# A decoder block on one core: when the first tile's expert rows are fetched

## The chip, the core and the metric

The kernel runs on one core of one Trainium2 chip. The metric is the device time of one execution in microseconds, median over runs. A core has a matrix engine (TensorE, PE in the profile; its weight loads are PEld), a vector engine (VectorE, DVE), an activation engine (ScalarE, ACT), a general engine (GpSimd, POOL) and a queue that only starts transfers (SyncE, SP). Each works through its own list of instructions in order. Where one instruction needs what another engine or a transfer makes, it waits, and all that stands behind it on its engine waits too.

## The reference, cut to what matters

One decoder layer on 512 tokens of width 1024, all in float32. The channel mixer at its end picks 128 experts for each token (8 heads with 16 each) out of 16384, and uses one row of u and one row of v for each:

```
h = rms_norm(x); proj = h @ w_in                # hgrn q,f,i,og | attn q,k,v | gate_a | gate_b
y_a = hgrn2_mixer(...);  y_b = dilated_attention_mixer(...)
merged = sigmoid(ga) * (y_a @ w_branch_a) + sigmoid(gb) * (y_b @ w_branch_b)
x = x + merged @ w_out
h2 = rms_norm(x)                                # peer_ffn(h2):
q = h2 @ w_q; scores against sub_keys; top 16 of 256 sums -> idx, gate = softmax(top scores)
hid = einsum('thkd,td->thk', u[idx], h2)        # 128 rows of u per token
a = gelu(hid) * gate
x = x + einsum('thk,thkd->td', a, v[idx])
```

## The kernel before

The 512 tokens are four tiles of 128. Tile 0 goes first and alone through the mixers, the output projection and the query projection; then tiles 1 to 3 go through the same steps together, as one `Front` with `split` set: each weight and each activation is cut into a high and a low half (line 98 on ACT makes the high half, line 99 the low one, on DVE or, one time in five among the w_in weights, on POOL), and each product is three matmuls (line 112).

The `Front` of tiles 1 to 3 runs these steps: the w_in products for HGRN2, attention and gates; `hgrn` and `attn` per tile; then `post`, which has four parts. W_AB multiplies the branch outputs by their weights, first all of branch a (line 479 into pairA), then all of branch b (line 479 into pairB, then line 481 and line 99 `xl<-pairA`). W_OUT is the output projection; line 494 adds its product to x, line 496 squares, line 500 sums, line 145 takes the reciprocal of the root. Line 512 then makes h2, three times: for tiles 1 and 2 in pairA, and for tile 3 in a buffer called h2g. Line 516 transposes h2 on PE, and W_Q is the query projection from it (line 112 again, `pp<-vs,wh`).

Weights stream through two buffers `w` of 512 KB (line 198, started by SP). After each such load the program calls `after_unit`, which for tiles 1 to 3 is `background`. This is where the work on tile 0's experts is put in.

For tiles 0 and 3 (`UG`), the rows of u are fetched one expert at a time: one indirect transfer started by POOL (line 648) brings 128 rows of 4 KB, one per token, into a buffer, and one DVE instruction (line 660) multiplies them by h2g and sums them into one column of `hid`. I call such a transfer of 512 KB with its product a row. A tile has 128 of them. There are four buffers, three named rq and one named row, used in turn. After the last row, line 664 (GELU, on ACT), line 665 and lines 553 to 557 (`thirds`) work the column sums up. `Pump` counts how many rows have been put in; `rows(n)` adds n to a credit and puts rows in until it is used up. The buffer h2g exists once: tile 3's h2 may be written into it when tile 0's last row has been multiplied.

A row of tile 0 has two conditions in the program of before: its buffer is free, and the load of weights with which it was put in has landed (`behind`, a dependence added by hand in `row`). Each load brings 1.8 rows; there are 50 loads of w_in and 16 in W_AB and W_OUT, and the rest of the 128 is put in by `before_h2`, ahead of line 512.

The order of instructions on each engine is set when the program is built, by a scheduler that takes the instructions whose inputs are ready by its own reckoning, in the order of the code where several are.

Of the kernel before, what the change touches and what calls it, by code (L numbers as in the profile page):

```python
# [18 lines left out]
P = 128  # L19
# [27 lines left out]

LPOOL = 5

ROWS_F = 1.8  # L50

NPRE, RING = 72, 56

# [20 lines left out]
def kernel(ctx: ExitStack, tc: tile.TileContext, x, wst, par, cst, cols, g2, keys, u, v, ut, vr, out):  # L74
# [22 lines left out]
    def halves(hi, lo, x, eng=None):  # L97
        nc.scalar.activation(hi, x, AF.Copy)  # L98
        (eng or nc.vector).tensor_tensor(out=lo, in0=x, in1=hi.bitcast(F32), op=ALU.subtract)  # L99
        return hi, lo  # L100
# [42 lines left out]
    def rstd_of(dst, ss, n):  # L143
        nc.scalar.activation(dst, ss, AF.Sqrt, bias=eps[:, 0:1], scale=1.0 / n)
        nc.vector.reciprocal(dst, dst)

    class Front:
# [318 lines left out]
                    for b in range(4):  # L466
                        nc.scalar.activation(dst[:, 2 * b:2 * b + 2], dst[:, 2 * b:2 * b + 2], AF.Sigmoid)

        def post(self, before_h2=lambda: None):

            ga, gb, N, n = self.ga, self.gb, self.N, self.n
            mT = ga
            if self.split:
                mT = [hp.tile([P, KC, NM], F32R, name=m)[:, :, :N] for m in ("hT", "xl")]
            for g, ks, y in ((ga, slice(0, 4), self.yaT), (gb, slice(4, 6), self.ybT)):
                for b in range(4):
                    c = slice(2 * b, 2 * b + 2)
                    for j, pt in self.proj_T(W_AB + b, y, ks):
                        nc.vector.tensor_mul(g[:, 2 * b + j], pt, g[:, 2 * b + j])
                    if g is gb:  # L480
                        (nc.vector if self.split else nc.gpsimd).tensor_tensor(out=ga[:, c], in0=ga[:, c], in1=gb[:, c], op=ALU.add)
                        if self.split:
                            halves(mT[0][:, c], mT[1][:, c], ga[:, c])
            g2b = fp.tile([P, 6 * S], F32, name="kT") if self.split else const.tile([P, KC * NU], F32, name="hL")
            g2b = g2b[:, :D]
            nc.sync.dma_start(out=g2b, in_=bass.AP(tensor=g2.tensor, offset=g2.offset, ap=[[0, P], [1, D]]))
            xt = hp.tile([P, NM // P, D], F32, name="pairB")[:, :n]
            ss = sp.tile([P, NM // P, 5], F32, name="ssx", bufs=1)[:, :n]
            scr = sp.tile([P, 256], BF16, name="scrx", bufs=1)
            nc.sync.dma_start(out=xt, in_=x[self.t0:self.t0 + N].rearrange("(t p) d -> p t d", p=P))  # L490
            for b in range(4):
                for ts, pt in self.proj_N(W_OUT + b, mT):
                    xs = xt[:, ts, b * 256:(b + 1) * 256]
                    nc.vector.tensor_add(xs, pt, xs)
                    for t in range(ts.start, ts.stop):
                        nc.scalar.activation(scr, xt[:, t, b * 256:(b + 1) * 256], AF.Square, accum_out=ss[:, t, b:b + 1])
                if b == 2:

                    nc.scalar.activation(root, ss[:, 0, b:b + 1], AF.Sqrt)
            nc.vector.tensor_reduce(out=ss[:, :, 4], in_=ss[:, :, :4], axis=AX.X, op=ALU.add)  # L500
            rstd_of(ss[:, :, 4], ss[:, :, 4], D)
            h2T = hp.tile([P, KC, NM], F32R if self.split else F32, name="vs")[:, :, :N]
            if self.split:
                h2T = h2T, hp.tile([P, KC, NM], F32R, name="xl")[:, :, :N]
                hu = self.hu = [const.tile([P, KC * NU], F32R, name=m).rearrange("p (k n) -> p k n", k=KC) for m in ("hH", "hL")]
            h2s = hp.tile([P, NM // P, D], F32, name="pairA")
            before_h2()
            for t, T in enumerate(self.tiles):
                h2 = h2s[:, t]
                if T in UG:  # L510
                    h2 = h2g[T] = const.tile([P, D], F32, name="h2g")
                self.last_h2 = nc.vector.scalar_tensor_tensor(h2, xt[:, t], ss[:, t, 4:5], g2b, op0=ALU.mult, op1=ALU.mult)
                for c in range(0, KC, 4):
                    pt = ps.tile([P, 4, P], F32, name="pt")
                    for k in range(4):
                        nc.tensor.transpose(pt[:, k], h2[:, (c + k) * P:(c + k + 1) * P], ident)
                    tk = slice(t * P, (t + 1) * P)
                    if self.split:
                        halves(*(h[:, c:c + 4, tk] for h in h2T), pt)
                    else:  # L520
                        nc.scalar.activation(h2T[:, c:c + 4, tk], pt, AF.Copy)
                    if T in UD:
                        d0 = UD.index(T) * P
                        halves(*(h[:, c:c + 4, d0:d0 + P] for h in hu), pt)

                nc.sync.dma_start(out=out[T * P:(T + 1) * P], in_=xt[:, t])
            rqs = [rq_pool.tile([P, PH, P], F32, name="rq") for _ in range(n)]
            for b in range(4):
                for j, pt in self.proj_T(W_Q + b, h2T):
                    for t in range(n):  # L530
                        nc.scalar.activation(rqs[t][:, 2 * b + j], pt[:, t * P:(t + 1) * P], AF.Copy)
            return rqs
# [109 lines left out]
    nrow, behind = [0], []  # L642
# [97 lines left out]
    rows, scat = Pump(), Pump()  # L740
# [4 lines left out]
    def mixers(f):  # L745
        f.proj_hgrn()
        for t in range(f.n):
            f.hgrn(t)
        f.proj_attn()
        for t in range(f.n):  # L750
            f.attn(t)
        f.proj_gates()

    f = Front(UG[:1], False, lambda load: None)
# [27 lines left out]
    row_places = [(rq_pool, "rq")] * 3 + [(gat, "row")]  # L782

    def background(load):
        behind[:] = [load]
        rows(min(ROWS_F, P - rows.done))

    f = Front(tuple(range(1, 4)), True, background)
    routing(0, rq0)
    rows.add(u_steps(UG[0]))  # L790
    mixers(f)
    rq1, rq2, rq3 = f.post(lambda: rows(2 * P))
    hH, hL = f.hu
    fctx.close()

# [129 lines left out]
def build(arrays):  # L925
    import concourse.bacc as bacc
    nc = bacc.Bacc("TRN2", target_bir_lowering=False, num_devices=1)
    args = {k: nc.dram_tensor(f"in_{k}_dram", a.shape, mybir.dt.from_np(a.dtype), kind="ExternalInput").ap()
            for k, a in arrays.items()}
    out = nc.dram_tensor("out_0_dram", (S, D), F32, kind="ExternalOutput").ap()  # L930
    with tile.TileContext(nc, schedule_with_timeline_sim=True) as tc:
        kernel(tc, **args, out=out)
    return nc
# [8 lines left out]
```

## Time and profile before

| | us |
|---|---|
| median of 3 runs | 1886.55 |
| lowest, highest | 1883.9, 1891.71 |
| the profiled execution | 1878.31 |
| its span | 1876.5 |
| PE busy in the span | 1684.9 (90%) |
| DVE busy | 1373.0 (73%) |
| ACT busy | 784.2 (42%) |
| POOL busy | 637.7 (34%) |

Between the profiled execution and its span lie 1.81 us. Times in the rows below count from the span's start. Tile 0's own front ends at about 200 us; the front of tiles 1 to 3, with tile 0's rows beside it, lasts from there to 664 us, and its query projection to 700 us. Then come the dense products with u (to about 1126 us) and those with v.

### The profile page before, as it was taken

The page shows a single profiled execution, that of the slowest core. Times are in us where ns is not written, and L with a number is a line of the kernel's source. Part 1 is how long each engine was busy: PE and PEld are TensorE (multiplying, and loading weights), DVE is VectorE, ACT ScalarE, POOL GpSimd, SP SyncE. Part 2 cuts the span into 40 slices and gives each one's busy share as a digit, 9 for nine tenths or more (in the row PEclk, how much of TensorE's full clock was granted, in tenths as well). Part 3 has the DMA queues.
Part 4 walks back from the last instruction along what each step waited for, and adds up shares of the span by engine and source line. Part 5 has one row for each costly group of instructions (what it writes and reads, how often), then busy time and mean ns, then how long its engine had stood idle before and what let it go on. Part 6 is the DMA issues. An engine that isn't in the chain of part 4 may idle for free.

```text
span 1876.5 us, 28078 instructions
## 1 busy us (share of the span) xinstructions
PE 1684.9 (90%) x10301; PEld 1496.5 (80%) x10301; DVE 1373.0 (73%) x2793; ACT 784.2 (42%) x1466; POOL 637.7 (34%) x502
## 2 busy tenths in 40 slices
PE   8998889788986599999999889999999999989995
PEld 7887888687775489988899778888888888877774
DVE  2114999956567748988899777787778877777874
ACT  3324443333342436662366793343334333323331
POOL 0000455732323301434444104433434334444431
PEclk9999989889997789999999869999999999999998
DMA  8776478766567724755666539999999988888885
GB/s 277 249 234 206 137 249 292 226 230 197 174 213 241 280 79 146 276 208 201 213 223 208 208 127 346 325 343 325 337 321 337 343 314 309 311 287 309 311 301 179
DMA packets 173386, 473.49 MB, mean 252 GB/s; under 512 B 14784, under 2 KB 62144, under 8 KB 173248
## 3 DMA queue, kind: packets, MB, share of 16 engines
q1 hardware_dynamic: 115840, 268.47, 41.9%
q0 software_dynamic: 55296, 201.35, 30.5%
q10 hardware_dynamic: 2112, 1.88, 0.3%
q8 instruction: 81, 1.33, 0.3%
q14 instruction: 57, 0.47, 0.1%
HBM read 442.80 MB, written 27.79 MB: 251 GB/s over the span
## 4 chain that ended last, share of the span: by engine, by line
PE 51%; DMA 24%; DVE 14%; issue 5%; ACT 3%; POOL 2%; DVEq 0%; ACTq 0%; POOLq 0%; SPq 0%
PE acc L873 19%; PE ph L112 15%; PE pp L112 10%; DMA Gc<-g_d 7%; DMA w<-in_wst_dram 6%; PE pg L711 5%; DMA rq<-in_u_dram,idx 4%; DMA row<-in_u_dram,idx 2%; DVE rq L660 2%; DVE wl L99 2%; DMA rowx<-in_u_dram,idx 2%; DMA rowx<-in_v_dram,idx 1%; DVE Gc L862 1%; ACT eg L705 1%; DVE row L660 1%
## 5 line engine op out<-in xcount | busy, mean ns | idle before, releaser
L873 PE MATMUL acc<-vl,ah 128*128 128x512 f32 x768 | 242.3, 395 | 8.2 <-DVE vl L869 8.1
L873 PE MATMUL acc<-vh,al 128*128 128x512 f32 x768 | 241.4, 392 | 0.0
L873 PE MATMUL acc<-vh,ah 128*128 128x512 f32 x768 | 224.7, 398 | 10.8 <-ACT vh L867 10.8
L648 POOL DMA_INDIRECT rowx<-in_u_dram,idx x96 | 125.0, 1302 | 221.0 <-ACT pre L822 61.6
L648 POOL DMA_INDIRECT rowx<-in_v_dram,idx x96 | 133.0, 1385 | 189.2 <-DVE h2g L679 90.8
L112 PE MATMUL ph<-hH,ul 128*128 128x256 f32 x640 | 183.5, 287 | 8.2 <-DVE ul L99 8.2
L112 PE MATMUL ph<-hH,uh 128*128 128x256 f32 x640 | 187.2, 293 | 3.6 <-ACT pre L822 3.6
L112 PE MATMUL ph<-hL,uh 128*128 128x256 f32 x640 | 183.1, 286 | 0.0
L112 PE MATMUL ph<-h,ub 128*128 128x256 f32 x768 | 178.3, 387 | 4.2 <-DMA ub<-in_ut_dram 4.1
L660 DVE SCALAR_TENSOR_TENSOR rq<-rq,h2g 128x1024 f32<-128x1024 f32 x96 | 128.1, 1338 | 66.6 <-DMA rq<-in_u_dram,idx 66.5
L873 PEld LDWEIGHTS acc<-vl,ah 128*128 128x128 f32 x768 | 144.3, 190 | 40.2 <-DVE vl L869 11.7
L98 ACT ACTIVATE ah<-Gc 128x384 fp32r<-128x384 f32 x128 | 67.0, 524 | 261.1 <-PE acc L873 255.9
L873 PEld LDWEIGHTS acc<-vh,ah 128*128 128x128 f32 x768 | 144.3, 191 | 39.6 <-ACT vh L867 12.2
L648 POOL DMA_INDIRECT rq<-in_u_dram,idx x96 | 108.6, 1132 | 196.9 <-DMA w<-in_wst_dram 71.0
L873 PEld LDWEIGHTS acc<-vh,al 128*128 128x128 f32 x768 | 145.0, 189 | 30.0
L98 ACT ACTIVATE uh<-ub 128x1024 fp32r<-128x1024 f32 x80 | 85.1, 1064 | 193.4 <-PE ph L112 154.8
L112 PEld LDWEIGHTS ph<-h,ub 128*128 128x128 f32 x768 | 146.1, 195 | 24.0 <-issue 4.7
L869 DVE TENSOR_TENSOR vl<-vb,vh 128x1024 fp32r<-128x1024 f32 x128 | 156.3, 1221 | 8.3 <-ACT vh L867 8.2
L711 PE MATMUL pg<-eg,e 128*128 128x128 bf16 x1152 | 147.1, 297 | 13.3 <-ACT eg L705 7.1
L867 ACT ACTIVATE vh<-vb 128x1024 fp32r<-128x1024 f32 x128 | 135.8, 1061 | 35.7 <-DMA vb<-in_vr_dram 34.7
L711 PEld LDWEIGHTS <-e 128*128 128x128 bf16 x1152 | 129.3, 119 | 25.4 <-DVE eg L701 9.8
L98 ACT ACTIVATE wh<-w 128x512 fp32r<-128x512 f32 x144 | 88.5, 628 | 141.8 <-PE pp L112 79.9
(292 smaller groups left out, 3949.5 us busy)
## 6 DMA issues: line engine op xcount, KB each, us to landing
ub<-in_ut_dram SPq DMA_DIRECT2D x128, 512.0 KB, 5.2
vb<-in_vr_dram SPq DMA_DIRECT2D x128, 512.0 KB, 7.0
w<-in_wst_dram SPq DMA_DIRECT2D x107, 512.0 KB, 4.9
g_d<-Gx SPq DMA_DIRECT2D x24, 960.0 KB, 4.3
Gc<-g_d SPq DMA_DIRECT2D x15, 1536.0 KB, 16.3
wh<-in_wst_dram SPq DMA_DIRECT2D x37, 256.0 KB, 5.2
wl<-in_wst_dram SPq DMA_DIRECT2D x33, 256.0 KB, 4.8
pairB<-in_x_dram SPq DMA_DIRECT2D x5, 512.0 KB, 5.3
```

The source lines that it names most:

```text
L98: nc.scalar.activation(hi, x, AF.Copy)
L99: (eng or nc.vector).tensor_tensor(out=lo, in0=x, in1=hi.bitcast(F32), op=ALU.subtract)
L112: nc.tensor.matmul(out, l, r, start=(k == 0 and i == 0), stop=(k == last and i == len(ops) - 1))
L648: d = nc.gpsimd.indirect_dma_start(out=r, out_offset=None, in_=src, in_offset=bass.IndirectOffsetOnAxis(ap=index, axis=0))
L660: nc.vector.scalar_tensor_tensor(r, r, 1.0, h2g[T], op0=ALU.mult, op1=ALU.mult, accum_out=hid[:, g, j:j + 1])
L705: nc.scalar.activation(eg[:, 2, :, q], e12[:, 1, :, q], AF.Copy, scale=pk3[:, VD.index(T), i + k + q:i + k + q + 1])
L711: nc.tensor.matmul(pt[:, q], e12[:, 0, :, q0 + q], eg[:, j, :, q0 + q], start=(j == 0), stop=(j == 2))
L862: nc.vector.tensor_mul(gsl[:, :ngu], a.rearrange("p (g t) -> p g t", t=GT), gsl[:, :ngu])
L867: behind[:] = [nc.scalar.activation(vH, vb, AF.Copy)]
L869: nc.vector.tensor_tensor(out=vL, in0=vb, in1=vH.bitcast(F32), op=ALU.subtract)
L873: nc.tensor.matmul(acc[t][c], l.rearrange("p g t -> p (g t)")[:, t * P:(t + 1) * P], r[:, c * 512:(c + 1) * 512], start=(b == 0 and i == 0 ...
```

## The change

Three edits. The dependence of a row on a load of weights is no longer set while tile 0's rows are put in. 2.8 rows go with each load instead of 1.8, so that the 128 rows are used up by the 46th of the 50 loads of w_in. And `rows(2 * P)`, which finishes the rows and adds the GELU and `thirds` of tile 0, stands between the mixers and `post`, instead of inside `post` ahead of h2. Line numbers of the changed program are lower by one from line 507 on, and by two after the edit at the end.

```diff
-ROWS_F = 1.8
+ROWS_F = 2.8
-        def post(self, before_h2=lambda: None):
+        def post(self):
             h2s = hp.tile([P, NM // P, D], F32, name="pairA")
-            before_h2()
             for t, T in enumerate(self.tiles):
     def background(load):
-        behind[:] = [load]
         rows(min(ROWS_F, P - rows.done))
     mixers(f)
-    rq1, rq2, rq3 = f.post(lambda: rows(2 * P))
+    rows(2 * P)
+    rq1, rq2, rq3 = f.post()
```

How the order of the instructions moves, at three places. First POOL, during attention: the starts of rows (L648 before, L647 after) and, between them, a low half that POOL makes (L99). In brackets stands what each waits for; DMAHW is a load by SP, DMASW an earlier row's landing, DVE the freeing of the buffer. Before:

```order
L99 TENSOR_TENSOR wl<-w,wh 128x512 [waits PE_49,Activation_49]
L648 DMA rq<-in_u_dram,idx 128x1024 [waits DMAHW6_49,DMASW2_49,DVE_49]
L648 DMA row<-in_u_dram,idx 128x1024 [waits DMASW3_49,DVE_49]
L648 DMA rq<-in_u_dram,idx 128x1024 [waits DMAHW7_49,DMASW4_49,DVE_49]
L648 DMA rq<-in_u_dram,idx 128x1024 [waits DMASW5_49,DVE_49]
L99 TENSOR_TENSOR wl<-w,wh 128x512 [waits PE_49,Activation_49]
```

The same place on POOL after:

```order
L99 TENSOR_TENSOR wl<-w,wh 128x512 [waits DMAHW4_49,PE_49,Activation_49]
L647 DMA row<-in_u_dram,idx 128x1024 [waits DMASW3_49,DVE_49]
L647 DMA rq<-in_u_dram,idx 128x1024 [waits DMASW4_49,DVE_49]
L647 DMA rq<-in_u_dram,idx 128x1024 [waits DMASW5_49,DVE_49]
L647 DMA rq<-in_u_dram,idx 128x1024 [waits DMASW6_49,DVE_49]
L647 DMA row<-in_u_dram,idx 128x1024 [waits DMASW7_49,DVE_49]
L99 TENSOR_TENSOR wl<-w,wh 128x512 [waits DMAHW6_49,PE_49,Activation_49]
```

No row waits for a load any more, and five rows stand between two low halves where four stood.

Second, DVE at the end of attention: L445 ends the last head of the last tile, L479 takes W_AB's products. Before:

```order
L445 TENSOR_SCALAR yb<-vg,m_4128 128x64
L479 TENSOR_TENSOR pairA<-pp,pairA 128x384
L99 TENSOR_TENSOR wl<-w,wh 128x512
L479 TENSOR_TENSOR pairA<-pp,pairA 128x384
L99 TENSOR_TENSOR wl<-w,wh 128x512
L660 SCALAR_TENSOR_TENSOR rq,hid<-rq,h2g 128x1024
L479 TENSOR_TENSOR pairA<-pp,pairA 128x384
```

The same place on DVE after:

```order
L659 SCALAR_TENSOR_TENSOR rq,hid<-rq,h2g 128x1024
L99 TENSOR_TENSOR wl<-w,wh 128x512
L479 TENSOR_TENSOR pairA<-pp,pairA 128x384
L445 TENSOR_SCALAR yb<-vg,m_4230 128x64
L659 SCALAR_TENSOR_TENSOR row,hid<-row,h2g 128x1024
L659 SCALAR_TENSOR_TENSOR rq,hid<-rq,h2g 128x1024
L99 TENSOR_TENSOR wl<-w,wh 128x512
L479 TENSOR_TENSOR pairA<-pp,pairA 128x384
```

Before the last L445, 94 rows stood on DVE; now 123 do. It comes after six of branch a's eight products instead of ahead of all of them, and 126 rows stand ahead of the last tile's `yb` halves.

Third, DVE between the end of W_OUT and W_Q: the sum of squares (L500), the reciprocal (L145), h2 (L512, after L511), its halves xl and hL (L99). Before:

```order
L500 TENSOR_REDUCE ssx<-ssx 128x3
L660 SCALAR_TENSOR_TENSOR rq,hid<-rq,h2g 128x1024
L145 RECIPROCAL ssx<-ssx 128x3
L512 SCALAR_TENSOR_TENSOR pairA<-pairB,ssx,kT 128x1024 x2
L660 SCALAR_TENSOR_TENSOR row,hid<-row,h2g 128x1024
L99 TENSOR_TENSOR xl<-pt,vs 128x4x128 x3
L99 TENSOR_TENSOR hL<-pt,hH 128x4x128
L660 SCALAR_TENSOR_TENSOR rq,hid<-rq,h2g 128x1024
L99 TENSOR_TENSOR hL<-pt,hH 128x4x128 x2
```

The same place on DVE after:

```order
L500 TENSOR_REDUCE ssx<-ssx 128x3
L145 RECIPROCAL ssx<-ssx 128x3
L511 SCALAR_TENSOR_TENSOR pairA<-pairB,ssx,kT 128x1024 x2
L511 SCALAR_TENSOR_TENSOR h2g<-pairB,ssx,kT 128x1024
L99 TENSOR_TENSOR xl<-pt,vs 128x4x128
L696 TENSOR_TENSOR e_6345<-iota,pk 128x1024
L696 TENSOR_TENSOR e_6367<-iota,pk 128x1024
L99 TENSOR_TENSOR xl<-pt,vs 128x4x128 x2
L700 TENSOR_TENSOR eg<-e_6345,pk 128x1024
L99 TENSOR_TENSOR hL<-pt,hH 128x4x128
L700 TENSOR_TENSOR eg<-e_6367,pk 128x1024
```

No row stands there any more, tile 3's h2 follows the other two at once, and four instructions of a later step (L696, L700) have moved in among the halves. In W_AB's branch b and in W_OUT no row is left either.

## Rows read from the trace of the kernel before

**Rows 1.** Busy us by stretch: PE, PEld, DVE, ACT, POOL; granted clock, DMA share, GB/s.

```profile
230.00:372.00 142.00, 116.55 (x826) 108.83 (x824) 135.76 (x280) 51.66 (x105) 89.00 (x66) 0.86 0.76 250
372.00:556.00 184.00, 163.11 (x1162) 143.22 (x1163) 111.31 (x225) 69.71 (x141) 56.18 (x55) 0.93 0.62 204
556.00:664.00 108.00, 63.52 (x380) 58.35 (x379) 82.05 (x135) 32.16 (x66) 32.88 (x29) 0.76 0.70 241
664.00:700.00 36.00, 36.00 (x197) 35.01 (x198) 10.65 (x19) 14.39 (x42) 0.00 (x0) 0.95 0.30 103
```

**Rows 2.** The chain of waits from 556 to 664 us, by line.

```profile
by line: DMA w<-in_wst_dram 24.9%; DMA rq<-in_u_dram,idx 24.8%; issue 12.4%; DVE rq L660 8.0%; DVE wl L99 5.6%; POOL rq L648 4.1%; DVE xl L99 3.7%; DVE row L660 2.3%; DVE pairA L512 2.3%; DVE h L830 2.0%; DVE hL L99 1.7%; DVE pairA L481 1.6
```

**Rows 3.** DVE's time in line 660 by stretch (two instructions each row), clock, DMA.

```profile
250.00:300.00 50.00, 23.85 (x40) 0.97 0.82 280
230.00:372.00 142.00, 67.78 (x100) 0.86 0.76 250
372.00:556.00 184.00, 57.59 (x91) 0.93 0.62 204
556.00:664.00 108.00, 38.83 (x64) 0.76 0.70 241
```

**Rows 4.** Waits from 372 to 556 us: total us, times, longest.

```profile
POOL rq L648 <- DMA w<-in_wst_dram: 50.7, 8, 8.4
POOL row L648 <- DMA w<-in_wst_dram: 14.7, 4, 6.6
...
DVE rq L660 <- DMA rq<-in_u_dram,idx: 47.4, 17, 5.1
DVE row L660 <- DMA row<-in_u_dram,idx: 10.9, 6, 3.7
```

**Rows 5.** Transfers from 300 to 372 us, then 372 to 430: size, median us to landing.

```profile
w<-in_wst_dram SPq DMA_DIRECT2D x8, 512.0 KB, 6.7
...
w<-in_wst_dram SPq DMA_DIRECT2D x10, 512.0 KB, 4.9
rq<-in_u_dram,idx POOLq DMA_INDIRECT x12, 5.8
```

**Rows 6.** POOL in order of time: start, us, what [idle before, releaser].

```profile
226.77 1.45 POOL L648 DMA_INDIRECT rq<-in_u_dram,idx  x1 [1.36 <-DVE rq L660]
```

**Rows 7.** PE in order of time, W_AB's branch b to W_Q.

```profile
558.46 0.51 PE L112 MATMUL pp<-yb,wh 128*128 128x384 f32 x2
...
578.67 0.47 PE L112 MATMUL pp<-wh,hT 128*128 128x256 f32 x1 [3.37 <-DVE pairB L479]
...
633.41 0.28 PE L112 MATMUL pp<-wh,xl 128*128 128x256 f32 x1
633.53 0.28 PE L112 MATMUL pp<-wl,hT 128*128 128x256 f32 x1
...
663.53 0.69 PE L112 MATMUL pp<-xl,wh 128*128 128x384 f32 x1 [1.32 <-DVE xl L99]
```

**Rows 8.** DVE in order of time, end of W_OUT to W_Q.

```profile
635.55 1.22 DVE L660 SCALAR_TENSOR_TENSOR rq<-rq,h2g 128x1024 f32<-128x1024 f32 x1
...
642.75 1.22 DVE L660 SCALAR_TENSOR_TENSOR rq<-rq,h2g 128x1024 f32<-128x1024 f32 x1 [2.94 <-DMA rq<-in_u_dram,idx]
...
644.11 2.48 DVE L512 SCALAR_TENSOR_TENSOR pairA<-pairB,ssx,kT 128x1024 f32<-128x1024 f32 x2
...
656.72 1.22 DVE L660 SCALAR_TENSOR_TENSOR row<-row,h2g 128x1024 f32<-128x1024 f32 x1
...
657.98 1.28 DVE L512 SCALAR_TENSOR_TENSOR h2g<-pairB,ssx,kT 128x1024 f32<-128x1024 f32 x1
...
659.38 2.29 DVE L830 TENSOR_TENSOR h<-hH,hL 128x2048 f32<-128x2048 f32 x1
661.59 1.29 DVE L697 TENSOR_TENSOR e<-iota,pk 128x1024 bf16<-128x1024 bf16 x2
```

**Rows 9.** ACT's wait for weights from 556 to 664 us.

```profile
ACT wh L98 <- DMA w<-in_wst_dram: 21.8, 7, 8.2
```

## The prediction

> **What bounds the kernel now.** I read the busy time by stretch first. The change touches only tile 0's rows, and they lie between 224 and 658 us, so I cut that time at the steps of the program. From 664 us on PE has no gap in the query projection [rows 1], so what the front gains or loses should reach the end. From 372 to 556 us (last w_in products, attention, gates, W_AB's branch a) PE is busy 163.1 of 184 us. From 556 to 664 us (branch b, W_OUT, h2) it is busy only 63.5 of 108 us [rows 1], at a granted clock of 0.76 in the mean, that is for about half of the time at the lower of its two levels, 1.2 GHz and not 2.4. These 44.5 idle us are the largest hole in the front.
>
> Then the chain of waits in this hole. A quarter of it is loads of weights, a quarter transfers of rq rows, a further tenth the product of rows on DVE; PE does not appear among its first eleven entries [rows 2]. So this stage is held up by things that DVE does in order between the operands that PE needs.
>
> Third, the waits of 372 to 556 us. POOL stood 50.7 + 14.7 = 65.4 us at the start of a row, until a load of weights had landed. DVE stood 47.4 + 10.9 = 58.3 us in front of a row's product, until the row had landed [rows 4]. DVE is busy 111.3 of 184 us there [rows 1], so 72.7 us are idle, and 58.3 of them are these waits: a row starts late, because it waits for a load, and is then waited for.
>
> **What the change moves.** Line 660 runs 91 times from 372 to 556 us and 64 times from 556 to 664 us; with two instructions a row that is 45.5 and 32 rows [rows 3]. In the order after, 29 more rows stand ahead of the last attention head, and no row is left behind the start of branch b but the last one or two. So the stretch from 372 us to branch b gets about 45.5 + 29 = 75 rows, and what follows up to W_Q none.
>
> **Part 1, the rows brought forward: +4 us.** One row costs DVE 57.6 / 45.5 = 1.27 us [rows 3], so 29 rows add 36.8 us to DVE's 111.3: 148 of 184 us. With the 14.4 us that DVE idles for other reasons (72.7 - 58.3) that is 162.5, and 21.5 us are left for waits on rows, 0.29 us each. Whether this holds depends on how fast four buffers can be turned over, now without the wait for a load. Floor: POOL starts a row 1.4 us after DVE has freed its buffer [rows 6], the row lands 5.8 us after its start [rows 5], DVE takes 1.27; that is 8.5 us for four buffers, 2.1 us a row, and 75 rows need 159 us. Slowest row of the trace: from 230 to 372 us, where most rows did not wait for a load, 50 rows went through in 142 us, 2.84 us each, but with DVE busy 135.8 of the 142 us [rows 1, 3]; 75 rows at that pace need 213 us. In between stands 250 to 300 us with 20 rows in 50 us, 2.5 us each [rows 3]. DVE has more room after 372 us than there, so I take 2.5: 75 x 2.5 = 187.5 us against 184, a cost of 4 us. The ends are kept: 159 us would leave PE as the bound, with its 163 us of work, so that at most some 10 us could be won; 213 us would cost 29. Transfers can carry it: 204 GB/s x 184 us is 37.5 MB, 29 rows of 0.524 MB add 15.2, and 52.7 MB in 188 us are 280 GB/s, as much as the transfers moved from 250 to 300 us, then at a share of 0.82 [rows 3].
>
> **Part 2, branch b: -3 us.** It lasts from 558.5 to 578.7 us [rows 7]. Eight products of 6 matmuls, at about the 0.17 us that one of 384 columns takes (half as much again as the 0.12 us of one of 256 [rows 7], an estimate), are 8 to 9 us of PE work. After the change the last rows and tile 0's GELU fall into its beginning, so I count 3 of the 20 us, with 0 and 8 as bounds.
>
> **Part 3, W_OUT: -14 us.** It lasts from 578.7 to 633.7, 55 us [rows 7]. Its 4 x 8 x 3 x 3 = 288 matmuls follow each other every 0.12 us at the full clock [rows 7], 34.6 us, which is the floor. The nearest stretch is the query projection behind it, the same eight loads of weights and no rows: 36 us with PE without a gap [rows 1]. I add 5 us, because unlike that one W_OUT begins with operands that DVE is still making (its first matmul had waited 3.4 us) [rows 7]: 41 us. Bounds are 36 and 55.
>
> **Part 4, from W_OUT to W_Q: -12 us.** From PE's last matmul at 633.7 to the query projection in earnest at 663.5 are 30 us [rows 7]. DVE has eight rows in there (the first at 635.55, the last at 656.72), 8 x 1.22 = 9.8 us, and one waits 2.9 us for its transfer while the reciprocal stands behind it [rows 8]. Line 512 for tile 3 comes 11.4 us after the other two began, because its buffer is tile 0's h2 and the last rows still read it. All that goes: 12.7 us. Line 830 (2.3 us) moves from ahead of the last xl to behind it, and four instructions of 0.65 us (half of the pair at 661.6) move ahead of it, two of which were ahead before [rows 8]: about -1. What is late next is the chain itself: sum, root, three h2, transposes, ten halves of 0.65 us. I take 12, with 8 and 15 as bounds.
>
> What I cost at nothing: the GELU's change of ACT table comes once more, but ACT is busy only 32 of 108 us there [rows 1], and PE has three buffers of products in front of it; uncovered I would not expect it to cost more than one row's product (1.2 us, an estimate). POOL starts the same 128 rows.
>
> **Sum.** 4 - 3 - 14 - 12 = -25 us. The profiled execution took 1878.31 (span 1876.5 and 1.8 around it); with 25 less it would take 1853. It lies 8.2 us below the median of the three runs, so against the median the forecast is 1886.55 - 25 = 1861.5 us.
>
> **Rivals.**
>
> First, the rows' pace becomes the bound. At 2.84 us a row part 1 costs 29 us, and 29 - 29 = 0: about 1886.5. For it: with 75 rows in order on DVE, attention's small steps and the low halves of weights stand behind each row that is not there yet, and eight products of branch a now stand among some thirteen rows. Against it: that pace was measured with DVE full of routing work [rows 1, 3].
>
> Second, slower. A row's wait on DVE stays what it was, 58.3 / 45.5 = 1.28 us, because the transfer itself is what takes long and not the wait ahead of it. Then 75 rows wait 96 us, and the stretch takes 162.5 + 96 = 258.5 us, 74.5 more; less 29 that is +45, about 1932. It decides from 0.67 us of wait a row on, where 162.5 + 75 x 0.67 = 213. For it: loads landed in 6.7 us instead of 4.9 when rows came densely [rows 5], so transfers do lengthen each other. Against it: from 230 to 372 us, where rows were hardly held back, DVE idled 6.2 us in all [rows 1], 0.12 us a row.
>
> The Trainium skill bears on this ("DMA: Bandwidth & Descriptors", section "Queues, rings and completion order"): each transfer engine goes round the queues that have work and changes between them only at whole packets, so a row and a load in flight together stretch each other. By that rule alone, with a row always beside a load, landing would go towards twice the undisturbed time, and this rival would be the forecast; the medians of 4.9 and 6.7 us agree in direction and are less than a doubling [rows 5].
>
> Third, only part 4 is won. ACT waited 21.8 us for weights between 556 and 664 us [rows 9]; if the loads, and not DVE, set the pace of branch b and W_OUT, parts 2 and 3 give nothing and -12 + 4 = -8 remains: about 1878.5. For it speaks the quarter of the chain that is loads [rows 2]; against it the same eight loads in the query projection, where PE had no gap [rows 1].
>
> **How the numbers follow.** The forecast gets 0.60, the first rival 0.17, the slower one 0.10, the third 0.13. What a measurement of this kernel can tell from no change is about 0.5%, 9.4 us. The forecast lies beyond it; a part of the third rival (0.06) does too, so faster gets 0.66, within 0.5% gets 0.23, slower 0.11 with a little from the first. The forecast's own range, with the bounds of its parts, goes from about 1845 (parts 2 to 4 at 6, 19, 14, part 1 at -3) to 1877. To leave out no more than two in ten the range must take in the third and most of the first: 1845 to 1888.
>
> **What the profile after would show.** Right: POOL's waits for loads of weights at row starts gone; the last row's product before about 562 us instead of 657; DVE's waits for rows between 372 and 560 us below some 30 us in sum; W_OUT in about 41 us with PE's clock near full; h2 of tile 3 directly behind the other two, and W_Q beginning near 638 us instead of 663. Wrong: attention and branch a ending 20 us or more later than at 558 us, with DVE waiting for rq and row transfers before every product; or W_OUT still lasting 50 us with ACT waiting for loads. The forecast would also fail if the dense stage behind 700 us gave the time back, which PE's full stretch at 664 us does not suggest.

## The result, and the profile after

| | before | after |
|---|---|---|
| median, us | 1886.47 (4 runs) | 1834.5 (4 runs) |
| lowest, highest | 1883.9, 1891.71 | 1826.47, 1845.72 |
| the profiled execution | 1878.31 | 1845.72 |
| its span | 1876.5 | 1843.9 |

The ratio is 0.9725, with a 95% interval from 0.967 to 0.9781: 52 us faster where 25 were forecast, and below the forecast's range (1845 to 1888). The two profiles differ by only 33 us, because that of before is of an execution quicker than any of the four timed ones, and that of after is the slowest of its four. A second profile of the changed kernel, taken with the experiments, is of an execution of 1830.23 us, 48 less than the profile of before. I use both.

The stages after, cut at the same steps of the program as in [rows 1] (w_in from 372 us on, branch a, branch b, W_OUT, from there to W_Q, W_Q; columns as there):

```profile
372.00:512.80 140.80, 135.43 (x1000) 121.23 (x998) 119.36 (x230) 54.82 (x119) 84.92 (x68) 0.97 0.88 302
512.80:553.40 40.60, 28.78 (x207) 24.62 (x205) 34.19 (x68) 16.68 (x29) 22.44 (x18) 0.83 0.88 297
553.40:567.40 14.00, 11.95 (x49) 10.86 (x49) 13.60 (x27) 6.87 (x10) 0.00 (x0) 0.76 0.48 157
567.40:608.80 41.40, 37.69 (x288) 36.42 (x288) 19.57 (x34) 17.17 (x38) 0.00 (x0) 0.96 0.44 141
608.80:623.50 14.70, 5.76 (x26) 4.75 (x25) 12.57 (x20) 9.44 (x25) 0.00 (x0) 0.63 0.42 143
623.50:659.60 36.10, 36.10 (x199) 34.88 (x198) 12.32 (x16) 12.43 (x35) 0.00 (x0) 0.96 0.30 103
```

And of before with the same cuts, w_in and W_OUT:

```profile
372.00:537.20 165.20, 145.90 (x1060) 126.93 (x1061) 99.03 (x202) 60.14 (x126) 49.64 (x49) 0.93 0.60 200
...
578.70:633.80 55.10, 42.78 (x288) 40.41 (x288) 38.32 (x62) 16.91 (x37) 16.91 (x15) 0.81 0.71 240
```

W_OUT takes 41.4 us instead of 55.1, and DVE has half as much to do in it. The w_in products end 24 us earlier on the clock of the trace, although DVE did more in them; PE stands still for 5 us there instead of 19, and its granted clock is 0.97 in the mean instead of 0.93. Branch a, though, takes 40.6 us instead of 21.3: the rows that were brought forward stand in it now.

The waits from 372 to 553 us after, against [rows 4] (total us, times, longest):

```profile
ACT wh L98 <- DMA w<-in_wst_dram: 44.3, 15, 7.7
POOL rq L647 <- DVE rq L659: 36.0, 28, 2.9
...
DVE rq L659 <- DMA rq<-in_u_dram,idx: 15.9, 15, 2.7
...
DVE row L659 <- DMA row<-in_u_dram,idx: 4.5, 5, 1.4
```

POOL waits for the freeing of buffers, and no longer for loads; DVE's waits for rows are 20.4 us, where they were 58.3. The largest entry is now ACT's wait for loads (20.1 us in the stretch of [rows 4]), whose transfers share the time with the rows'.

DVE's time in a row's product after, against [rows 3], and the transfers from 378 to 512 us, against [rows 5]:

```profile
378.00:512.00 134.00, 74.28 (x111) 0.97 0.89 305
372.00:550.00 178.00, 99.22 (x153) 0.94 0.87 300
```

```profile
w<-in_wst_dram SPq DMA_DIRECT2D x22, 512.0 KB, 7.2
rq<-in_u_dram,idx POOLq DMA_INDIRECT x42, 6.8
row<-in_u_dram,idx POOLq DMA_INDIRECT x14, 6.5
```

153 instructions in 178 us are 76.5 rows, one each 2.33 us. Loads and rows land later than before, at a DMA share of 0.89. In the second profile, from 378 to 510 us, the delay is smaller:

```profile
w<-in_wst_dram SPq DMA_DIRECT2D x22, 512.0 KB, 6.2
rq<-in_u_dram,idx POOLq DMA_INDIRECT x42, 6.4
row<-in_u_dram,idx POOLq DMA_INDIRECT x13, 6.1
```

The end of W_OUT on DVE after, against [rows 8] (start, us, what, idle before and its releaser), and the start of W_Q on PE, against [rows 7]:

```profile
611.71 0.17 DVE L500 TENSOR_REDUCE ssx<-ssx 128x3 f32<-128x12 f32 x1 [1.12 <-ACT scrx L496]
612.25 0.18 DVE L145 RECIPROCAL ssx<-ssx 128x3 f32<-128x3 f32 x1 [0.36 <-ACT ssx L144]
612.46 2.48 DVE L511 SCALAR_TENSOR_TENSOR pairA<-pairB,ssx,kT 128x1024 f32<-128x1024 f32 x2
614.86 1.28 DVE L511 SCALAR_TENSOR_TENSOR h2g<-pairB,ssx,kT 128x1024 f32<-128x1024 f32 x1
```

```profile
623.45 1.01 PE L112 MATMUL pp<-vs,wh 128*128 128x384 f32 x2
```

The third h2 stands directly behind the first two.

What scatters from run to run is mostly outside the stages of the change. From W_Q's end to the end of the span there are 1176.7 us in the profile of before, 1184.3 and 1173.8 in the two of the changed kernel, and 1169 to 1192 in those of the experiments. So I compare profiles by one length, the front: from the first product of a tile 0 row to the end of W_Q. Before it is 475.4 us (224.4 to 699.8), after 429.7, and in the second profile 429.1. The change gave 46 us in there. Most kernels below have one profile each, so how far the front of one program scatters is known only from these two. That the medians differ by 52 has nothing in these stages to show for the last 6 us; the profiled run of before lies 8 us under its median.

### The profile page after: what moved, and what is told of

It reads as the page before. It is cut to its first block, busy times and chain, and to the rows that moved or that the text cites. A ratio compares the mean times of both kernels' runs of the same rounds, so it can differ in the third digit from the quotient of the medians.

```text
span 1843.9 us, 28097 instructions
## 1 busy us (share of the span) xinstructions
PE 1672.6 (91%) x10301; PEld 1485.2 (81%) x10301; DVE 1374.9 (75%) x2793; ACT 783.4 (42%) x1467; POOL 653.9 (35%) x502
## 4 chain that ended last, share of the span: by engine, by line
PE 49%; DMA 23%; DVE 18%; issue 5%; ACT 3%; POOL 2%; DVEq 0%; SPq 0%; POOLq 0%; ACTq 0%
PE acc L872 16%; PE ph L112 13%; PE pp L112 12%; DMA Gc<-g_d 7%; PE pg L710 5%; DMA w<-in_wst_dram 3%; DMA row<-in_u_dram,idx 3%; DMA rq<-in_u_dram,idx 3%; DMA rowx<-in_u_dram,idx 2%; DVE rq L659 2%; DVE wl L99 1%; DVE row L659 1%; DVE Gc L861 1%; DMA rowx<-in_v_dram,idx 1%; DVE h2g L678 1%
## 5 line engine op out<-in xcount | busy, mean ns | idle before, releaser
L647 POOL DMA_INDIRECT rowx<-in_v_dram,idx x96 | 136.3, 1420 | 204.1 <-DVE h2g L678 93.4
L647 POOL DMA_INDIRECT rowx<-in_u_dram,idx x96 | 125.9, 1312 | 215.8 <-issue 57.0
L647 POOL DMA_INDIRECT rq<-in_u_dram,idx x96 | 118.6, 1236 | 99.3 <-DVE rq L659 62.4
```

Of the source, the lines that this page charges most:

```text
L647: d = nc.gpsimd.indirect_dma_start(out=r, out_offset=None, in_=src, in_offset=bass.IndirectOffsetOnAxis(ap=index, axis=0))
```

## The experiments

The change does three things at once: it takes away a wait, it puts more rows behind each load, and it moves `rows(2 * P)`. The order on the engines moves with them. Theory A: the gain comes from where the rows stand in the order (the prediction's parts 3 and 4). Theory B: it comes from the waits for loads themselves. The expectations name these, and C and D for the rows that are left.

| run | rows a load | waits for loads | rows on DVE at last head | front, us | ratio to before, 95% |
|---|---|---|---|---|---|
| before | 1.8 | yes | 94 | 475.4 | 1 |
| e3_rest_before_post | 1.8 | yes | 96 | 464.8 | 0.9942 (0.9914 to 0.9969) |
| w20_wait_2 | 2.0 | yes | 110 | 446.9 | 0.9851 (0.9807 to 0.9895) |
| e2_wait_28 | 2.8 | yes | 123 | 430.0 | 0.9700 (0.9666 to 0.9735) |
| n1_order_of_before | 1.8 | no | 96 | 441.7 | 0.9765 (0.9731 to 0.98) |
| v20_no_wait_2 | 2.0 | no | 108 | 423.7 | 0.9691 (0.9653 to 0.973) |
| e1_no_wait | 1.8 | no | 123 | 436.4 | 0.9725 (0.9687 to 0.9763) |
| a_again (the change) | 2.8 | no | 123 | 429.1 | 0.9704 (0.967 to 0.9738) |

The edit of n1 and v20 reaches further than the others. It stands in `row`, which tile 3 uses too, behind 700 us, with rows that wait for a result of ACT. POOL's largest waits of that kind before, from 700 to 1830 us:

```profile
POOL rowx L648 <- ACT pre L822: 68.8, 21, 10.5
POOL rowx L648 <- ACT ah L98: 40.0, 16, 11.8
```

In n1 and v20 no such wait is left. So their ratios hold more than tile 0's rows, and what the wait for loads cost is read from their fronts.

### Each edit alone

**e1_no_wait.** The dependence alone is removed:

```diff
     def background(load):
-        behind[:] = [load]
```

> Only the dependence on loads is removed; still 1.8 rows with each load, and the last rows put in ahead of line 512. Each engine's order comes out as in the changed kernel (123 rows ahead of the last attention head, none behind branch b). Theory A (the gain comes from where the rows stand in the order: none in branch b, W_OUT and ahead of h2): as fast as the changed kernel, 0.972 of before, -52 us; W_OUT in about 41 us. Theory B (it comes from the turnover of the four buffers, which the waits for loads slowed): the same, -52 us, since the waits are gone. Rival C (the larger credit, 2.8, is what brings the rows forward): 1.0 of before, W_OUT in about 55 us.

Measured 1838.23 us, 0.9725. This edit alone gives the change's order and, within the intervals, its gain (39 of the 46 us of the front). Theories A and B both expected that; rival C falls.

**e2_wait_28.** Only the number of rows:

```diff
-ROWS_F = 1.8
+ROWS_F = 2.8
```

> Only 2.8 rows with each load instead of 1.8; the rows still wait for their load, and rows(2 * P) stands where it stood before. DVE's order is that of the changed kernel. Theory A (order): W_OUT about 41 us, no row ahead of h2, most of the gain: -40 to -52 us. Theory B (turnover): a row's wait on DVE stays 1.28 us as before; by the prediction's second rival 75 rows then wait 96 us and the stretch from 372 us to branch b takes about 258 us instead of 184: slower than before by up to 45 us in sum, or at best 0 if half of the waits go.

Measured 1831.37 us, 0.9700: also the whole gain, with the dependence on loads still in the program. Theory B expected a loss or nothing. The waits of POOL from 372 to 556 us in this run:

```profile
POOL rq L648 <- DVE rq L660: 38.5, 27, 3.3
...
POOL row L648 <- DVE row L660: 9.7, 7, 2.0
```

No wait for a load is left among them, where before had 65.4 us [rows 4]. With 2.8 rows a load the four buffers cannot keep up, rows fall behind, and the load that a row names has landed before its buffer is free. So this run brings the rows forward and loses the waits at once, as the change does, and does not tell theory A from B.

**e3_rest_before_post.** Only the third edit:

```diff
-    rq1, rq2, rq3 = f.post(lambda: rows(2 * P))
+    rows(2 * P)
+    rq1, rq2, rq3 = f.post()
```

> Only rows(2 * P) is moved to between the mixers and post; 1.8 rows with each load, each behind its load, as before. DVE has 96 rows ahead of the last head (before 94), 119 by W_OUT's beginning and all 128 by its end; none stands ahead of h2. By the prediction's part 4: -12 us, W_OUT still near 55 us. If the waits for loads were what cost the stretch up to branch b 19 us (the run without waits in the order of before), POOL's waits stay near 65 us from 372 to 556 us and nothing is won there. If -30 us or more come, the waits were not it, but the order alone.

Measured 1875.62 us, 0.9942, 11 us less, as part 4 had it (12). W_OUT and the stretch behind it in its profile:

```profile
586.50:640.70 54.20, 43.38 (x289) 41.20 (x289) 41.52 (x74) 20.75 (x44) 19.85 (x15) 0.81 0.79 274
640.70:656.40 15.70, 5.71 (x25) 4.74 (x25) 12.83 (x22) 10.63 (x26) 0.00 (x0) 0.61 0.38 134
```

No row stands ahead of h2, and the 30 us to W_Q have become 16. W_OUT, with 17 rows in it, has hardly moved. Up to branch b it took 7 us longer than before (340.9 us from the first row's product, 334.0 before); the front is 11 us shorter in sum. POOL still waited for loads, 47 us:

```profile
POOL rq L648 <- DMA w<-in_wst_dram: 37.2, 7, 8.4
...
POOL row L648 <- DMA w<-in_wst_dram: 9.8, 2, 6.7
```

### Order and wait apart

**n1_order_of_before.** The dependence stays for the scheduler, so that each row is placed behind its load, but nothing waits for it on the chip:

```diff
-                mybir.DependencyClass.Sync, mybir.DependencyReason.DATA), reason="a row's turn")
+                mybir.DependencyClass.NoSync, mybir.DependencyReason.DATA), reason="a row's turn")
```

> The kernel before with the same order rule (each row is still put in behind its load by the scheduler: 96 rows ahead of the last head, before 94; 122 rows by the end of W_OUT, last row ahead of tile 3's h2), but no row waits for a load on the chip. Theory A (order): the waits of POOL (65 us from 372 to 556 us) and most of DVE's waits for rows (58 us there) go, yet W_OUT stays at 50 us or more and the stretch from W_OUT to W_Q near 30 us, so 0 to -15 us of the 52. Theory B (turnover): DVE has no waits left in W_OUT and h2 either, -25 us or more, with W_OUT at 45 us or less.

Measured 1840.21 us, 0.9765, 46 us less, with as many rows in W_OUT (16) as before and seven still ahead of tile 3's h2. In the front, where the edit touches the wait for loads alone, it is 34 us. Theory A expected 15 at most. Of theory B's two signs the time came, and W_OUT at 45 us or less did not (49). The same stages in its profile (w_in, branch a, branch b, W_OUT, to W_Q):

```profile
372.00:518.00 146.00, 140.97 (x1071) 122.89 (x1070) 105.51 (x212) 57.21 (x122) 64.70 (x54) 0.98 0.72 246
518.00:540.00 22.00, 18.56 (x122) 17.77 (x121) 14.78 (x28) 14.24 (x23) 5.06 (x6) 1.00 0.62 198
540.00:555.00 15.00, 10.12 (x51) 8.09 (x49) 13.94 (x26) 3.36 (x6) 6.42 (x6) 1.00 0.92 322
555.00:604.00 49.00, 41.07 (x288) 39.53 (x288) 37.58 (x63) 17.13 (x37) 19.41 (x17) 0.83 0.81 276
604.00:629.90 25.90, 6.79 (x29) 5.46 (x28) 24.31 (x38) 11.37 (x23) 3.80 (x3) 0.57 0.56 216
```

POOL waited for the freeing of buffers from 372 to 556 us and not for loads, and DVE's waits for rows are 18.4 us, where they were 58.3:

```profile
POOL rq L648 <- DVE rq L660: 38.3, 20, 9.8
...
DVE rq L660 <- DMA rq<-in_u_dram,idx: 13.7, 8, 4.0
...
DVE row L660 <- DMA row<-in_u_dram,idx: 4.7, 3, 4.1
```

The w_in stretch falls from 165.2 to 146.0 us, and PE's idle time in it from 19.3 to 5.0. Branch b loses 5 us, W_OUT 6, the stretch to W_Q 4. The order is not word for word that of before (96 rows for 94, and rows and low halves change places here and there), so a little of this may be order.

**w20_wait_2 and v20_no_wait_2.** Both have 2.0 rows a load, the first with the wait, the second with the edit of n1. Their orders are nearly the same (110 and 108 rows ahead of the last head, the last row among the same products of W_OUT). The difference is the wait (behind 700 us that of tile 3's rows too).

```diff
-ROWS_F = 1.8
+ROWS_F = 2.0
```

> No wait on the chip, order rule of before, and 2.0 rows with each load: between the run without waits in the order of before and the changed kernel. 108 rows ahead of the last head (123 in the changed kernel, 96 in that run), 122 at W_OUT's beginning, all by its end. If rows in branch a cost (15 us more there for some ten rows more) what rows in W_OUT cost (7.5 us for 16 rows), it ends level with the changed kernel, 0.970; if rows cost least in W_OUT where DVE is half idle, it gains 3 to 8 us on it; theory A, by which no row may stand in W_OUT, has it 3 to 8 us behind.

> The kernel before with 2.0 rows a load instead of 1.8, waits for loads kept: almost the order of the run with 2.0 and no wait (110 rows ahead of the last head against 108, last row at the same place), 47 of the rows with a wait for a load in the program. It asks from which credit on the wait stops costing. If a wait costs because a row is put in just behind its load while a buffer stands free, a little more credit keeps the buffers full and the loads ahead: near the run without the wait, 0.97 of before, and POOL's waits for loads from 372 to 556 us fall from 65 us to under 15. If the waits of 1.8 are still there in proportion (47 of 54), -15 us at most, from the order alone (rows(2 * P) moved alone gave -11).

Measured 0.9691 without the wait and 0.9851 with it. In the front the wait cost 23 us (446.9 against 423.7). In the run with it, POOL and DVE waited from 372 to 556 us:

```profile
POOL rq L648 <- DMA w<-in_wst_dram: 38.3, 7, 10.1
...
DVE rq L660 <- DMA rq<-in_u_dram,idx: 36.5, 22, 4.7
```

So it fades more slowly than I had expected (under 15 us). POOL's waits for loads of 65 us (47 in e3), 38 and 0 at 1.8, 2.0 and 2.8 rows a load go with 34, 23 and 1 us of the front that the wait costs (475.4 against 441.7, 446.9 against 423.7, 430.0 against 429.1).

v20_no_wait_2 has the lowest median of all complete kernels, 1826.18 us, and its front is 5 us shorter than the change's, but the intervals overlap: not shown to be faster. Its branch b, W_OUT and the stretch behind it:

```profile
537.70:549.20 11.50, 9.99 (x49) 7.92 (x48) 11.50 (x22) 3.27 (x5) 4.08 (x5) 1.00 0.80 255
549.20:601.50 52.30, 41.34 (x290) 39.90 (x289) 39.44 (x69) 20.56 (x43) 13.06 (x11) 0.80 0.73 251
601.50:616.10 14.60, 5.66 (x25) 4.70 (x24) 12.50 (x19) 9.33 (x25) 0.00 (x0) 0.62 0.41 144
```

W_OUT takes 52 us, near the 55 of before, and the whole is no slower than the change: what the rows take here they do not take in branch a, 22.7 us in this run (PE 515.2 to 537.9) and 34 in the second profile of the change (511.0 to 545.1).

**a_again.** The change once more.

> The changed kernel once more, for a second profile of it. All theories: 0.967 to 0.978 of before. If the 46 us that its first profile gained up to W_Q are the change's own, this one shows the end of branch a again about 11 us earlier, W_OUT at 41 us and 15 us from W_OUT to W_Q; if what it lost behind W_Q (some 8 us) and in tile 0's front (5.6 us) was chance, it does not come back here.

Measured 1831.24 us, 0.9704. Its w_in products end at 511.2 us, W_OUT takes 41.6 and the stretch behind it 14.6; tile 0's first row is back at 225.6 and the tail at 1173.8 us. What the first profile lost there did not come back: it varies from run to run (the first row's product starts between 224.4 and 232.0 us in all these profiles).

### What the rows still cost

**z_no_rows.**

```diff
         g = UG.index(T)
-        for j in range(P):
+        if g == 0:
+            nc.vector.memset(hid[:, g], 1.0)
+        for j in range(P if g else 0):
```

> The changed kernel without tile 0's rows of u: their 128 transfers and products are left out, hid of tile 0 is set to 1 (so tile 0's output is another one). It tells what the rows still cost in the changed kernel. Theory C (brought forward and without waits, the rows lie almost wholly in time that PE needs anyway): the stretch from 372 us to branch b, 176 us in the second profile of the changed kernel, falls to PE's own 163 us, branch b and W_OUT stay at 14 and 41 us; in sum 15 us off the front from 372 us on. Theory D (the row pace is still the bound of that stretch, as in the prediction's part 1): 176 us falls by 25 us or more, because the low halves and attention's steps on DVE no longer stand behind rows. Either way the 146 us from 225 to 372 us may fall too, to no less than PE's 116.

Measured 1764.91 us, 66 less than the change (1831.24): theory C, by which rows lie in covered time, falls. W_Q ends at 589.7 us instead of 654.7. Its w_in and branch a:

```profile
372.00:475.30 103.30, 103.30 (x891) 89.73 (x890) 43.30 (x102) 50.94 (x104) 6.38 (x5) 1.00 0.28 87
475.30:491.80 16.50, 16.50 (x97) 16.50 (x96) 8.30 (x15) 6.20 (x10) 0.00 (x0) 1.00 0.31 98
```

PE has no gap and its full clock. After the change the 128 rows cost 66 us. Before they cost 121 (1886.28 - 1764.91), if the kernel before without them took the same time, which was not run. By this the change took away a little under half of what they cost.

**p3_three_buffers.** The changed kernel with

```diff
-    row_places = [(rq_pool, "rq")] * 3 + [(gat, "row")]
+    row_places = [(rq_pool, "rq")] * 3
```

> The changed kernel with three buffers for the rows instead of four (the buffer named row is left out of the turn). If the turnover of the buffers sets the pace (theory D: 1.4 + 6.9 + 1.3 = 9.6 us from a buffer's being free to its being free again, by four 2.4 us a row, by three 3.2), the 59 rows that went through from 372 to 511 us take 0.8 us more each, 47 us, and rows slide back into W_OUT: slower than the changed kernel by 20 us or more. If transfers as a whole or DVE set it (theory C), the pace stays near 2.4 us and the time within 10 us of the changed kernel.

Measured 1867.17 us, 0.9897, 36 more than the change; 21 of it is in the front. The products of rows in its w_in stretch:

```profile
372.00:526.60 154.60, 71.32 (x109) 0.93 0.79 262
```

and in the second profile of the change:

```profile
372.00:511.00 139.00, 77.05 (x117) 0.96 0.89 308
```

54.5 rows at 2.84 us against 58.5 at 2.38: 0.46 us more, between theory D's 0.8 and theory C's nothing; the whole, 36 us, is as theory D had it.

The traces tell why. A buffer's turn lasts from the end of the product that frees it to the end of the next product in it, four rows later (three here). In the mean over the w_in stretch, worked out from the starts of rows on POOL and their products on DVE:

| | turn, us | until POOL starts the row | until DVE starts its product | product |
|---|---|---|---|---|
| before | 15.6 | 8.5 | 5.8 | 1.3 |
| the change, second profile | 9.5 | 0.8 | 7.4 | 1.3 |
| three buffers | 8.5 | 0.6 | 6.7 | 1.3 |

Before, a buffer stood empty for more than half of its turn; in the other two it is filled again almost at once, and a turn shared among four or three buffers is the pace, 2.4 and 2.8 us. Of the change's 7.4 us the row's landing takes 6.5, where the trace tells it, and a landed row waits 0.9 for DVE. So the turnover sets the pace in both, and what theory D had wrong is that a turn stays 9.6 us: with three buffers it is 1.0 us shorter. Whether the rows land sooner there or wait less for DVE stays open, because the trace of that run lacks their landings. What the other 15 us behind the front are, I have not followed.

### x for the output projection

**k1_x_by_tile and v20_x_by_tile.** In the chain of waits of the change, the load of x into pairB holds 9% between 511 and 604 us. It was cut into three transfers, in the changed kernel and in that of v20_no_wait_2:

```diff
-            nc.sync.dma_start(out=xt, in_=x[self.t0:self.t0 + N].rearrange("(t p) d -> p t d", p=P))
+            xr = x[self.t0:self.t0 + N].rearrange("(t p) d -> p t d", p=P)
+            for t in range(n):
+                nc.sync.dma_start(out=xt[:, t], in_=xr[:, t])
```

> The changed kernel with x for the output projection loaded by three transfers of 512 KB, one a tile, instead of one of 1.5 MB, so that the first sum of W_OUT (tiles 1 and 2) need not wait for the third tile. In the changed kernel this transfer is 9% of the chain from 511 to 604 us. If it holds PE, W_OUT falls from 41.6 to about 38 us, the 37.9 of the run without rows: -3 us. If the chain's entry is only beside PE's work, no change within 0.4%.

> No wait on the chip, 2.0 rows a load in the order rule of before, and x by tile: the fastest run so far (1826 us) with the split of x. Rows stand in its W_OUT, which takes 52 us with DVE's low halves as what PE waits for, not x; so no change from that run, 0.969 of before, within 0.4%; 3 us better if x holds W_OUT here too.

Measured 0.9746 (0.971 to 0.9783) and 0.972 (0.9679 to 0.976): no gain on 0.9704 and 0.9691 that can be told from none. W_OUT in the first did fall to 39.3 us:

```profile
559.10:598.40 39.30, 36.24 (x288) 34.93 (x288) 19.62 (x34) 17.24 (x38) 0.00 (x0) 1.00 0.45 149
```

Inconclusive: two or three us are below what these runs resolve.

## Why the prediction was wrong

**Part 1, the rows brought forward, failed.** It said +4 us for the stretch up to branch b; measured from the first row's product, this stretch went from 334.0 us to 323.4 and 322.3, 11 us less. In the words of the prediction: "DVE has more room after 372 us than there, so I take 2.5". The pace was 2.33 us a row in the profile after: 75 rows at that pace are 175 us instead of 187.5. The 2.5 was read from a stretch in which DVE had less room, so the sentence itself spoke for a quicker pace. That it could go faster than 2.5 was in the bounds, and the floor of 159 us was worked out there; a turn took 9.5 us and not the floor's 8.5, with rows that landed after 6.5 us in the mean and not 5.8.

Behind the size lies something that I had left out: the wait was a cost by itself. The prediction worked the price of 29 more rows, and gave nothing to the 45 rows that were there already, though it had read their 58 us of waits on DVE. n1_order_of_before does the one without the other. Its first row's product and its first product of branch b (before: 224.43 and 558.46):

```profile
225.03 2.06 DVE L660 SCALAR_TENSOR_TENSOR rq<-rq,h2g 128x1024 f32<-128x1024 f32 x1
...
540.08 0.51 PE L112 MATMUL pp<-yb,wh 128*128 128x384 f32 x2
```

The stretch between them is 315.1 us, 19 less than before. Against it the change, with 26 more rows before branch b (76 for 50 from 372 us on), needs 322 to 323, and e1_no_wait, in the change's order, 330.3. So the rows brought forward cost 7 to 15 us, at least the forecast's 4; ten more rows instead of 26 cost nothing there (309.2 in v20_no_wait_2). The missing term is the 19.

Of the 27 us between forecast and measurement, part 1 explains 15 and parts 2 and 4 three each. For the last 6 no stage shows a cause.

**Parts 2 and 4 were right in kind and too small.** Branch b gave 6 us (3 forecast), the stretch from W_OUT to W_Q 15 (12, and 15 was its bound). e3_rest_before_post shows part 4's mechanism alone. The prediction's part 4 says that tile 3's h2 comes 11.4 us after the other two began; that is from their end, and 13.9 from their beginning [rows 8], but the sum does not use it. **Part 3** was met: W_OUT 41.4 us, 41 forecast. Yet in n1_order_of_before, with the rows left in these stages, 5 of branch b's 6 us came too, 6 of W_OUT's 14 and 4 of the 15 behind it. These parts are in some measure the wait's, which the prediction put down to the rows' place.

**But the parts do not say where the gain is from.** The forecast got 29 us from placing the rows and next to none from the waits. Without the wait and with the rows left where they were, 34 of the front's 46 us are won; with the wait in the program and more rows a load, all of it, because the wait then never comes last. The place of the rows, once no row waits, is worth 5 to 18 us of the front: 441.7 in the order of before, 423.7 and 429.1 with 12 and 27 more rows ahead of the last head, 436.4 in e1_no_wait; as e1 and the change differ by 7 us in the same order of rows, the lower end is not shown to be more than nothing. A row costs time in branch a as it does in W_OUT.

**The rivals.** The first (2.84 us a row) did not come: the change had 2.33 to 2.38, and 2.84 came with three buffers. The second, slower one decided from 0.67 us of wait a row on; the measured one is 20.4 us for some 76 rows, 0.27 us. Transfers did lengthen each other: rows landed in 6.1 to 6.8 us in the two profiles instead of 5.2 to 5.8, loads in 6.2 and 7.2 instead of 4.9. By the Trainium skill ("DMA: Bandwidth & Descriptors", section "Queues, rings and completion order") an engine takes turns between the queues that have work, packet by packet. The trace agrees in direction, but rows rose by a quarter at most and loads by a quarter to a half, not to the double. The third rival (loads set the pace of W_OUT) is refuted by W_OUT itself: 41 us, in which no wait of ACT for weights was among the nine longest.

**What the profile was to show.** POOL's waits for loads are gone; the last row's product ended at 559 us (562 forecast); DVE's waits for rows are 20 us (below 30); W_Q began at 623.5 instead of 638, earlier by the 15 + 3 + 3 us that parts 1, 2 and 4 were off, and later by the 5.5 us by which tile 0 was late in this profile.

What stays open: why the tail varies by up to 24 us between runs, why e1_no_wait has a front 7 us longer than the change in the same DVE order of rows, what makes a buffer's turn shorter with three buffers than with four, and what the waits of tile 3's rows are worth, which n1 and v20 drop as well. A fifth buffer was not tried.

## What to carry to other kernels

When a chain of waits shows one engine at a transfer's start and another at its landing, price the removal for the work that is there already, before the work that is moved. A dependence that only paces a stream cost next to nothing here while the stream lagged behind it (1 us at 2.8 rows a load) and 34 us where the stream had caught up (1.8); raising the rate by half removed the wait as well as deleting it. To tell order from wait, keep the dependence in the scheduler and drop it on the chip, and see which other instructions the same edit reaches.

## What the runs showed of the hardware

With up to four row transfers and the weight loads in flight and no wait between them, the transfers' share rose from 0.60 to 0.88 and the throughput from 200 to 302 GB/s over the w_in stretch. A row's product on DVE became a little longer in the mean: 74.28 us for 55.5 rows, 1.34 us, where it was 1.27; the median of the multiplication stayed 1.22. Over the w_in stretch PE's granted clock was higher where PE had fewer gaps: 0.93 in the mean with 19 us of idle time, 0.97 and 0.98 with 5, and 1.00 without rows, where there were none. A short stretch by itself need not follow this: branch b had 1.00 with 4.9 of 15 us idle in n1_order_of_before, and 0.76 with 2.1 of 14 after the change.
